# A decoder step on one core: the first group's gather of the last tiles in float32, and sums over partition quarters in quarters of the array

## The chip, the cores and the metric

The kernel runs on one NeuronCore of a Trainium2 chip. The metric is the device time of one execution in microseconds (us). Three runs of the kernel before took 421.94, 422.75 and 424.46 us; the median is 422.75. All rows of before below are of one profiled execution.

## The reference, cut to what matters

One layer of a decoder is computed for 256 prompt tokens and for 8 new tokens, each of which has 1024 cached keys and values in pages.

```python
xn = rmsnorm(x, g_mix); proj = xn @ w_in                     # 1024 -> q | k | v | B | C | h, 512 each
q, k = rope(q), rope(k)                                      # 8 heads of 64
att  = moba_attend(q, k_all, v_all, pos)                     # blocks of 256 keys: own block + top 3 past ones
conv_out, _ = short_conv(c_gate * h_in, conv_prev, conv_w)   # 3 taps
hres = x + concat([att, b_gate * conv_out]) @ w_out          # 1024 -> 1024
hn   = rmsnorm(hres, g_ffn)
# router: best of 4 groups, best 2 of its 8 experts, gates = softmax of the two x probability of the group
h = silu(einsum('td,edf->tef', hn, w_gate)) * einsum('td,edf->tef', hn, w_up) * gates   # 32 experts, 256 wide
y = rmsnorm(hres + einsum('tef,efd->td', h, w_down), g_final)
```

Outputs are the normed rows of both token sets, their keys and values, and the state of the convolution. All is float32.

## The kernel before, in words

Tokens are tiled as tile 0 and tile 1 (128 prompt tokens each) and tile 2 (the 8 new tokens, on 8 partitions). The work ahead of the experts is cut into some 300 named steps. The string `ORDER` lists them; each engine runs its instructions in that order. Q, K, S are steps over the cached keys (gathered by POOL's indirect DMA, multiplied by DVE or POOL, summed by DVE), V over the cached values, `o` the output projection, `H`, `l`, `L` the second norm and the router's logits, `ra` to `re` the five parts of the routing of a tile, `rk` and `oh` the rank of a token within its expert and the one-hot matrix `Pg`, `g` the gather matmuls, `ga` and `gt` copies and transposes of the gathered rows. The first digit behind a letter is mostly the tile.

A product with the 8 new tokens uses TensorE in four column quarters (`mm_quad`, L243): quarter c takes contraction rows of one chunk, and its result is on partitions 32c to 32c+7. The four partial results are then added by a matmul with the 0/1 matrix `sel8`, whose 8 columns pick partitions 0 to 7 of every quarter (`samp_sum` L263, `out_sum` L773; `sq`, `sk`, `sv`, `y0`, `y1` in the order).

The cached values: for token b, `pv_mm` (L709, steps V0 to V7) sums values by probabilities in the four quarters. A DVE multiplication keeps of each of 8 rows its own head (L713). `pv_sum` (L718, X0 and X1) adds the quarters with the matrix `strip`. `pe` adds the token's own value, `as` (L744) transposes.

Expert weights stream through SP's queue into a ring of slots: two `c9` (once `xnT`, `mixT`), nine `rk` (once cached keys and values), four `rw` (once the weights of the projections). Experts are done four at a time, 32 token slots each, in eight groups: `pgt` (gate), `pup` (up, L1149), `px` (gather for the next group), `pyy` (down, L1163), `pz` (scatter). A weight request waits until its slot has been read for the last time, and all behind it in SP's queue wait too. Two `u` tiles of group 0 are loaded in pieces into free small tiles (`load_split`, L1081; their place is taken in step `room`).

The gather of rows is a matmul with the one-hot `Pg`. For it the rows of the residual `yres` are kept as a high part `hn` (float32r, cast by ACT, L820) and a low part `hlo` (the rest, L827: by POOL for tile 2, by DVE for the others), both in an order of columns that makes 8 chunks of every eighth column. Each half of a gather (`PX`, 512 columns) takes a float32r matmul of the high and one of the low part of tiles 0 and 1, and one for tile 2, whose low part lies on partitions 32 to 39 of the same tile:

```python
n = 40 if t == 2 else 128                                   # L985
for low in lows[:1] if t == 2 else lows:
    T.matmul(PX[grp, hf], lhsT=PgS[grp][:n, POS[t]].rearrange("p j s -> p (j s)"), ...
```

Steps `warm0` to `warm2` (L1063) are matmuls without use for the result between the steps that wait for the ranks.

Of the kernel before, what the change touches and what calls it, by code (L numbers as in the profile page):

```python
# [22 lines left out]
H = 8  # L23
# [25 lines left out]
C_ROPE, C_SEL, C_IOTA, C_W4, C_W8, C_WT, C_W = 0, 96, 104, 136, 140, 148, 152  # L49


def _table():
# [12 lines left out]
    t[:, C_WT:C_WT + 4] = [1, 2, 3, 4]  # L65
    return t
# [19 lines left out]
def hymba_step(ctx: ExitStack, tc: tile.TileContext, x_prompt, x_sample, cache_k, cache_v, state_conv,  # L86
# [35 lines left out]
    with tc.manual_schedule():  # L122
# [173 lines left out]
        norm1_T(0)  # L296
        idx = small("idx", [128, 8, 2], I32)
# [28 lines left out]
        strip = small("strip", [128, 64])  # L326
# [27 lines left out]
        def _():  # L354
# [4 lines left out]
            P.memset(strip, 0.0)  # L359
            P.memset(strip[:, 31:32], 1.0)  # L360
# [329 lines left out]
        def _():  # L690
# [5 lines left out]
            for g in range(2):  # L696
                V.tensor_tensor(pvs[g][:, :, :, 0:8], Sd[:, 4 * g:4 * g + 4],
                                bc(rden)[:, 4 * g:4 * g + 4], op=OP.mult)
# [3 lines left out]
        def pv_mm(b):  # L702
            if b == 0:
                Pd["pa"] = ps("pa")
            po = ps("pov", "qb")
            for s in range(2):
                for j in range(4):
                    i = 2 * j + s
                    T.matmul(po[32 * j:32 * j + 32], lhsT=pvs[b // 4][:, b % 4, i, :],  # L709
                             rhs=vslots[2 * b + i // 4][:, i % 4, :], start=s == 0, stop=s == 1,  # L710
                             tile_position=(0, 32 * j))
            mks[b] = c2("mk", [128, 512])
            V.tensor_tensor(mks[b].rearrange("p (h d) -> p h d", h=8), po.rearrange("p (h d) -> p h d", h=8),  # L713
                            sel8[:, :, None].to_broadcast([128, 8, 64]), op=OP.mult)

        def pv_sum(b):
            j = b % 4
            T.matmul(Pd["pa"][32 * j:32 * j + 32], lhsT=strip[:, 31 - b:63 - b], rhs=mks.pop(b),  # L718
                     start=b < 4, stop=b >= 4, tile_position=(0, 32 * j))

        for b in range(8):
            steps[f"V{b}"] = lambda b=b: pv_mm(b)
        steps["X0"] = lambda: [pv_sum(b) for b in range(4)]
        steps["X1"] = lambda: [pv_sum(b) for b in range(4, 8)]

        @step("pe")
        def _():
# [7 lines left out]
            attq = c2("attq", [128, 512])  # L735
            S.copy(attq, Pd["pa"])
            V.tensor_tensor(attq[0:8], attq[0:8], aself, op=OP.add)
            Pd["attq"] = attq
# [57 lines left out]
        def norm2_half(t, k):  # L796
# [20 lines left out]
            V.tensor_tensor(xh[t][:, c0:c0 + m, 0:n], pv_[:, 0:m, 0:n],  # L817
# [591 lines left out]
```

## Time and profile before

| what | us |
|---|---|
| median of three runs | 422.75 |
| the profiled execution, whole | 423.49 |
| its span, first to last instruction | 421.8 |
| PE busy in the span | 382.7 (91%) |
| DVE busy | 196.4 (47%) |
| POOL busy | 104.7 (25%) |
| ACT busy | 92.0 (22%) |

The core moved 155.04 MB by DMA, 119.69 MB of it through SP's queue. A row of a timeline gives start and length in us, engine, line, operation, the tiles written and read, the shape and how many instructions it merges; what stands in brackets is the engine's idle time just before it and what ended it. PE is TensorE's matmuls; in float32 each matmul is two instructions, in float32r one.

### The profile page before, as it was taken

How to read it: one execution, taken by the hardware profiler on the slowest of the kernel's cores; microseconds unless marked ns; L12 is line 12 of the kernel's file. 1: busy time of each engine (PE TensorE's matmuls, PEld its weight loads, DVE VectorE, ACT ScalarE, POOL GpSimd, SP SyncE). 2: the span in 40 equal slices, each digit the busy share in tenths (PEclk: the TensorE clock that was granted, in tenths of full speed). 3: DMA queues.
4: the chain of work that ended last, by engine and by line, in shares of the span. 5: the costliest groups of instructions: out<-in, count | busy, mean ns of one | idle time of the engine just before them, and what ended most of it. 6: DMA issues, size and time to landing. Idle time of an engine off the chain costs nothing.

```text
span 421.8 us, 6576 instructions
## 1 busy us (share of the span) xinstructions
PE 382.7 (91%) x2626; PEld 208.0 (49%) x2626; DVE 196.4 (47%) x384; ACT 92.0 (22%) x232; POOL 104.7 (25%) x103
## 2 busy tenths in 40 slices
PE   7899999999999999987999999888699699799980
PEld 6354346678775334464545554443353364354530
DVE  2148987899764033688234343406015016024054
ACT  4120223164340012241320212111011021011032
POOL 3636888978306001030100000000000000000041
PEclk9899999999999999999899999989889789799996
DMA  7999978869987999949699999999999999999922
GB/s 259 416 373 421 367 292 308 340 220 392 424 358 266 421 429 423 409 204 347 234 413 399 425 427 425 426 428 424 428 427 424 427 427 426 427 427 416 401 99 108
DMA packets 32981, 155.04 MB, mean 368 GB/s; under 512 B 3068, under 2 KB 5322, under 8 KB 17972
## 3 DMA queue, kind: packets, MB, share of 16 engines
q1 hardware_dynamic: 27328, 119.69, 70.1%
q0 software_dynamic: 5008, 33.80, 20.3%
q10 hardware_dynamic: 612, 1.11, 0.7%
q8 instruction: 22, 0.36, 0.3%
q14 instruction: 11, 0.09, 0.1%
HBM read 152.40 MB, written 2.20 MB: 367 GB/s over the span
## 4 chain that ended last, share of the span: by engine, by line
PE 42%; DMA 32%; DVE 13%; issue 7%; POOL 3%; ACT 1%; DVEq 0%; ACTq 0%; SPq 0%; POOLq 0%
DMA u<-in_w_up_dram 14%; DMA g<-in_w_gate_dram 9%; DMA d<-in_w_down_dram 8%; PE py L755 4%; PE pup L1149 4%; PE pov L709 3%; PE acck L238 3%; DVE Sd L480 3%; PE accB L552 3%; PE pgt L1149 3%; PE accq L238 3%; PE pyy L1163 3%; PE accv L238 2%; PE px L987 2%; POOL K L474 1%
## 5 line engine op out<-in xcount | busy, mean ns | idle before, releaser
L1149 PE MATMUL pup<-u,xg 128*32 128x256 f32 x472 | 42.9, 468 | 12.2 <-DMA u<-in_w_up_dram 12.2
L1223 DVE SCALAR_TENSOR_TENSOR sh<-pup,rsl,sh 128x256 f32<-128x256 f32 x8 | 5.3, 666 | 90.2 <-PE pup L1149 83.6
L1126 POOL TENSOR_TENSOR PGw<-Pg,G 128x384 f32<-128x384 f32 x8 | 6.9, 857 | 161.0 <-DVE Pg L976 124.4
L474 POOL TENSOR_TENSOR K<-K,qv 128x2048 f32<-128x2048 f32 x9 | 40.7, 4536 | 6.3 <-DMA K<-in_cache_k_dram,idx 4.5
L480 DVE TENSOR_REDUCE Sd<-K 128x32 f32<-128x2048 f32 x16 | 35.9, 2277 | 4.7 <-POOL K L474 4.6
L1149 PE MATMUL pgt<-g,xg 128*32 128x256 f32 x512 | 32.5, 394 | 3.5 <-DMA g<-in_w_gate_dram 2.4
L1149 PEld LDWEIGHTS pup<-u,xg 128*32 128x32 f32 x472 | 19.2, 133 | 32.0 <-DMA u<-in_w_up_dram 16.3
L1163 PE MATMUL pyy<-d,hT 128*32 128x512 f32 (+1 forms) x272 | 30.9, 579 | 0.6 <-DVE hT L1243 0.6
L755 PE MATMUL py<-wo,mixT 128*128 128x512 f32 (+1 forms) x72 | 29.0, 550 | 1.1 <-DVE yres L760 1.1
L1180 PE MATMUL pz<-Y,PT 128*128 128x512 f32 (+1 forms) x90 | 26.7, 421 | 0.7
L1149 PEld LDWEIGHTS pgt<-g,xg 128*32 128x32 f32 x512 | 16.5, 113 | 18.4 <-DMA g<-in_w_gate_dram 3.8
L1257 DVE TENSOR_TENSOR yres<-yres,pz 128x512 f32<-128x512 f32 (+1 forms) x42 | 25.6, 670 | 0.0
L1172 DVE SCALAR_TENSOR_TENSOR Y<-pyy,gsl,Y 128x512 fp32r<-128x512 f32 (+1 forms) x17 | 12.2, 720 | 25.5 <-ACT Y L1171 25.5
L998 ACT COPY xr<-px 128x512 f32<-128x512 f32 (+1 forms) x16 | 8.8, 557 | 68.0 <-PE px L987 68.0
L987 PE MATMUL px<-hn,Pg 128*128 128x512 f32 (+1 forms) x48 | 21.9, 480 | 0.1
L1171 ACT ACTIVATE Y<-pyy,gsl 128x512 fp32r<-128x512 f32 (+1 forms) x17 | 11.3, 663 | 48.3 <-PE pyy L1163 48.3
L1180 PEld LDWEIGHTS pz<-Y,PT 128*128 128x128 f32 (+1 forms) x90 | 12.1, 154 | 18.0 <-ACT Y L1171 6.4
L303 POOL DMA_INDIRECT V<-in_cache_v_dram,idx x16 | 15.1, 944 | 22.2 <-PE pov L709 18.2
L755 PEld LDWEIGHTS py<-wo,mixT 128*128 128x128 f32 x72 | 13.3, 190 | 13.5 <-issue 11.8
L303 POOL DMA_INDIRECT K<-in_cache_k_dram,idx x16 | 15.7, 982 | 12.4 <-DMA K<-in_cache_k_dram,idx 5.6
L1163 PEld LDWEIGHTS pyy<-d,hT 128*32 128x32 f32 x272 | 8.3, 111 | 17.7 <-issue 16.1
L238 PE MATMUL accq<-wq,xnT 128*128 128x512 f32 x32 | 16.3, 657 | 0.3 <-DVE xnT L221 0.3
(334 smaller groups left out, 612.0 us busy)
## 6 DMA issues: line engine op xcount, KB each, us to landing
g<-in_w_gate_dram SPq DMA_DIRECT2D x32, 1024.0 KB, 19.6
d<-in_w_down_dram SPq DMA_DIRECT2D x28, 1024.0 KB, 19.6
u<-in_w_up_dram SPq DMA_DIRECT2D x25, 1024.0 KB, 19.5
u<-in_w_up_dram SPq DMA_DIRECT2D x9, 512.0 KB, 14.2
wo<-in_w_out_dram SPq DMA_DIRECT2D x4, 1024.0 KB, 15.1
wk<-in_w_in_dram SPq DMA_DIRECT2D x2, 1024.0 KB
wv<-in_w_in_dram SPq DMA_DIRECT2D x2, 1024.0 KB, 30.6
wC<-in_w_in_dram SPq DMA_DIRECT2D x2, 1024.0 KB
```

The source lines that it names most:

```text
L238: T.matmul(acc, lhsT=xnT[:, cc, 128 * t:128 * t + 128], rhs=W[pn, kk][:, c, :], start=cc == 0, stop=cc == 7)
L303: P.indirect_dma_start(out=t, out_offset=None, in_=src, in_offset=bass.IndirectOffsetOnAxis(ap=idx[:, b, hh:hh + 1], axis=0))
L474: P.tensor_tensor(kslots[i], kslots[i], qv[:, None, :].to_broadcast([128, 4, 512]), op=OP.mult)
L480: V.tensor_reduce(Sd[:, b, 4 * hh:4 * hh + 4, :].rearrange("p i h -> p (i h)"), kslots[i].rearrange("p i (h d) -> p (i h) d", h=8), axis=A ...
L552: T.matmul(acc[:, 0:264], lhsT=W[pn, kk][:, c, 128 * m:128 * m + 128], rhs=xnT[:, cc, 0:264], start=cc == 0, stop=cc == 7)
L709: T.matmul(po[32 * j:32 * j + 32], lhsT=pvs[b // 4][:, b % 4, i, :], rhs=vslots[2 * b + i // 4][:, i % 4, :], start=s == 0, stop=s == 1, t ...
L755: T.matmul(po[:, lo:lo + w], lhsT=mixT[:, c, 128 * t:128 * t + 128], rhs=wo[n, c // 4][:, c % 4, lo:lo + w], start=c == 0, stop=c == 7, sk ...
L987: T.matmul(PX[grp, hf], lhsT=PgS[grp][:n, POS[t]].rearrange("p j s -> p (j s)"), rhs=(hn, hlo)[low][t][:n, 4 * hf:4 * hf + 4, :].rearrange ...
L1149: T.matmul(dst[32 * j:32 * j + 32, 0:256], lhsT=xg[:, c, 32 * j:32 * j + 32], rhs=w[:, 256 * k:256 * k + 256], start=c == 0, stop=c == 7, ...
L1163: T.matmul(py[32 * j:32 * j + 32, 0:w], lhsT=hT[:, c, 32 * j:32 * j + 32], rhs=dw[grp, j][:, 1024 * c + a:1024 * c + b], start=c == 0, sto ...
L1180: T.matmul(pz, lhsT=PTS[grp][:, 128 * t:128 * t + NR[t]], rhs=Y[:, i, 0:w], start=start and i == 0, stop=i == 1, skip_group_check=more)
L1257: V.tensor_tensor(yv, yv, pz[:m], op=OP.add)
```

## The change

Six things are changed together.

1. Sums over quarters (`sum_quarters`): the 512 columns are cut into four pieces of 128, and the sum of piece j is done in column quarter j of the array, so that the results stand on partitions 32j to 32j+7. Four copies (or adds) of 128 columns take them back.
2. Four new tokens share one result of the value products: the probabilities of token b of a group of four lie in columns 8(b%4) to 8(b%4)+7 of their 32, and 4 x 16 instructions add into one PSUM tile. One mask multiplication follows for a group. A new step `pa` sums the quarters for both groups; `pe0`, split off `pe`, computes the own value's part earlier; `as` transposes directly.
3. The first group's gather of tiles 2 and 1 reads `yres` itself in float32 (step of 8 elements), with `Pg` as float32, instead of `hn` and `hlo`. The high and low parts of these tiles are made in new steps `hl2`, `hl1` at the end of the order, for the later groups.
4. The order: `re0` comes before the projection of the new tokens, `re2` and `re1` behind the gather, `g00` and `g01` earlier, `R1` ahead of the last scaling of tile 1's transposed rows (`H12` is cut into `H12a`, `H12b`).
5. Three fill steps of two matmuls become one of two and one of one; two matmuls (`keep_warm(2)`) are added behind the first norm's transposes.
6. The two split `u` tiles are requested before the last `g` tile of group 1 instead of behind it.

```diff
@@ ORDER
-cv2 b3 B10 b2 V3 cv0 V0 c2 c3 ov V2 V1 B13 eB1 G25 o010 kvs o000 eB3 G26 eB0 G27 G28 G29 o110 G30 V5 eB2 X0 V4
-o001 V6 H00 G31 o011 V7 H01 X1 pe l00 o100 R0 l01 L0 ra0 rb0 O00 rc0 o101 as rk0 O01 co rd0 z0 z1 y0 oh0 H10 y1 H20
-H21 l20 R2 g00 O20 l21 O21 L2 ra2 rb2 room g01 o111 rc2 l10 O10 o112 H11 R1p H12 rk2 oh2 R1 O11 l11 l12 L1 ra1 rb1 rc1
-g20 warm0 g21 warm1 rk1p rk1 warm2 oh1 O12 rd2 g10h g11h re0 g10l ga0 g11l ga1 re2 gt0 gt1 rd1 re1
+cv2 b3 B10 b2 V3 cv0 V0 c2 c3 ov V2 V1 B13 eB1 G25 o010 kvs pe0 o000 eB3 G26 eB0 G27 G28 G29 o110 G30 V5 eB2 V4
+o001 V6 H00 G31 o011 V7 H01 l00 pa pe o100 R0 l01 L0 ra0 rb0 O00 rc0 o101 as O01 co rd0 re0 z0 z1 rk0 oh0 y0
+y1 H10 g00 H20 g01 H21 l20 R2 l21 L2 ra2 rb2 room o111 rc2 l10 o112 H11 R1p H12a R1 H12b rk2 oh2 l11 l12 L1 ra1 rb1 rc1
+g20 warm0 g21 rk1p rk1 warm1 oh1 rd2 g10 ga0 g11 ga1 gt0 gt1 rd1 re2 re1 hl2 hl1
@@ quarters
+        def sum_quarters(acc, x):
+            for j in range(4):
+                T.matmul(acc[32 * j:32 * j + 8, 0:128], lhsT=sel8, rhs=x[:, 128 * j:128 * j + 128], start=True, stop=True,
+                         tile_position=(0, 32 * j))
...
-            T.matmul(sm[0:8], lhsT=sel8, rhs=part[pn], start=True, stop=True)
-            S.copy(samp[pn], sm[0:8])
+            sum_quarters(sm, part[pn])
+            for j in range(4):
+                S.copy(samp[pn][:, 128 * j:128 * j + 128], sm[32 * j:32 * j + 8, 0:128])
...
         norm1_T(0)
+        keep_warm(2)
@@ values
+            if left[g] == 0:
+                mks[g] = c2("mk", [128, 512])
+                V.tensor_tensor(mks[g].rearrange("p (h d) -> p h d", h=8), po.rearrange("p (h d) -> p h d", h=8),
+                                tab[:, C_HEAD:C_HEAD + 8, None].to_broadcast([128, 8, 64]), op=OP.mult)
...
+        @step("pa")
+        def _():
+            Pd["pa"] = ps("pa")
+            for j in range(4):
+                for g in range(2):
+                    T.matmul(Pd["pa"][32 * j:32 * j + 8, 0:128], lhsT=tab[:, C_TOK + 4 - 4 * g:C_TOK + 12 - 4 * g],
+                             rhs=mks[g][:, 128 * j:128 * j + 128], start=g == 0, stop=g == 1,
+                             tile_position=(0, 32 * j))
...
-                T.matmul(pat[:, 8 * c:8 * c + 8], lhsT=Pd["attq"][:, 128 * c:128 * c + 128], rhs=sel8, start=True,
-                         stop=True)
+                T.transpose(pat[:, 8 * c:8 * c + 8], Pd["attq"][:, 128 * c:128 * c + 128], ident[0:8, 0:8])
@@ output rows of the new tokens
-            T.matmul(po2[0:8], lhsT=sel8, rhs=yq[n], start=True, stop=True)
-            yv = yres[0:8, 2, 512 * n:512 * n + 512]
-            V.tensor_tensor(yv, yv, po2[0:8], op=OP.add)
+            sum_quarters(po2, yq[n])
+            for j in range(4):
+                yv = yres[0:8, 2, 512 * n + 128 * j:512 * n + 128 * j + 128]
+                V.tensor_tensor(yv, yv, po2[32 * j:32 * j + 8, 0:128], op=OP.add)
@@ gather
+                if grp == 0 and t:
+                    n = NR[t]
+                    T.matmul(PX[grp, hf], lhsT=fl(PgS[grp], t, n).bitcast(F32),
+                             rhs=yres[:n, t, :].rearrange("t (p c) -> t c p", c=8)[:, 4 * hf:4 * hf + 4, :],
+                             start=False, stop=t == 1)
+                    continue
...
-            steps[f"warm{i}"] = lambda: fill(2)
+            steps[f"warm{i}"] = lambda i=i: fill(2 - i)
@@ SP's queue
+                    if (grp, nm, j) == (1, "g", 3):
+                        for k in (2, 3):
+                            load_split(0, "u", k, uw, wu_v)
...
-                if (grp, nm) == (1, "g"):
-                    for j in (2, 3):
-                        load_split(0, "u", j, uw, wu_v)
```

## Rows read from the trace of the kernel before

**Rows 1.** The page's 40 slices of the span: GB/s that the DMA engines moved

```profile
GB/s 259 416 373 421 367 292 308 340 220 392 424 358 266 421 429 423 409 204 347 234 413 399 425 427 425 426 428 424 428 427 424 427 427 426 427 427 416 401 99 108
```

**Rows 2.** Busy time by stretch; at the end granted clock, DMA share, GB/s

```profile
184.00:189.00 5.00, 3.86 (x22) 3.17 (x21) 4.69 (x14) 1.03 (x3) 1.67 (x2) 1.00 0.07 26
...
199.00:203.00 4.00, 2.87 (x28) 1.30 (x30) 3.26 (x20) 1.42 (x7) 0.00 (x0) 0.61 0.97 406
203.00:207.00 4.00, 4.00 (x55) 2.50 (x47) 0.71 (x3) 0.59 (x2) 1.02 (x1) 0.96 0.09 28
...
223.00:400.00 177.00, 160.56 (x1432) 83.24 (x1430) 51.52 (x86) 24.01 (x53) 5.00 (x6) 0.92 1.01 424
```

**Rows 3.** Timeline of SP's queue, 174 to 230 us: start, length, request

```profile
175.03 14.14 SPq L1110 DMA_DIRECT2D g<-in_w_gate_dram  x4
...
206.90 13.93 SPq L1110 DMA_DIRECT2D d<-in_w_down_dram  x4
```

**Rows 4.** The chain that ended last, 195 to 245 us: start, length, what

```profile
200.48 5.03 PE pgt L1149 x64
...
207.72 3.59 PE pup L1149 x64
211.31 3.29 PE px L987 x10
...
216.91 3.69 PE pyy L1163 x32
```

**Rows 5.** Timeline of PE

```profile
46.84 1.92 PE L243 MATMUL acck<-wk,xnT 128*32 128x512 f32 x16
...
147.70 1.04 PE L718 MATMUL pa<-mk,strip 128*32 128x512 f32 x8
148.56 1.90 PE L709 MATMUL pov<-V,Pp 128*32 128x512 f32 x16
...
156.37 3.60 PE L755 MATMUL py<-wo,mixT 128*128 128x512 f32 x8
...
162.34 1.37 PE L718 MATMUL pa<-mk,strip 128*32 128x512 f32 x8
...
177.36 1.02 PE L773 MATMUL py<-yq,tab 128*8 128x512 f32 x2
...
186.81 1.99 PE L755 MATMUL py<-wo,mixT 128*128 128x256 f32 x8 [1.14 <-DVE yres L760]
```

**Rows 6.** Timeline of DVE

```profile
182.63 0.24 DVE L862 SCALAR_TENSOR_TENSOR L<-pl,rsb,biasb 8x36 f32<-8x36 f32 x1 [0.67 <-POOL rsb L858]
...
186.20 0.23 DVE L914 SCALAR_TENSOR_TENSOR rcols<-rcols,tab 128x8 f32<-128x8 f32 x1
...
191.83 0.25 DVE L862 SCALAR_TENSOR_TENSOR L<-pl,rsb,biasb 128x36 f32<-128x36 f32 x1 [0.40 <-POOL rsb L858]
...
193.49 0.23 DVE L914 SCALAR_TENSOR_TENSOR rcols<-rcols,tab 128x8 f32<-128x8 f32 x1
...
195.32 0.29 DVE L976 TENSOR_TENSOR Pg<-rka,tab 128x128 fp32r<-128x128 f32 x1
...
198.01 0.74 DVE L1000 COPY xr<-px 128x256 f32<-128x256 f32 x2
```

**Rows 7.** Groups by line and shape, 175 to 192 us: busy, mean ns of one

```profile
L827 POOL TENSOR_TENSOR hn<-yres,hn 8x512 fp32r<-8x512 f32 x2 | 3.0, 1515 | 0.1
...
L827 DVE TENSOR_TENSOR hlo<-yres,hn 128x512 fp32r<-128x512 f32 x1 | 1.1, 1085 | 0.0
...
L827 DVE TENSOR_TENSOR hlo<-yres,hn 128x256 fp32r<-128x256 f32 x1 | 0.6, 610 | 0.0
```

**Rows 8.** Timeline of PE, the first 20 us

```profile
1.44 4.78 PE L287 MATMUL warm<-ident 128*128 128x128 f32 x24 [1.44 <-POOL ident masks.py:199]
...
8.57 3.70 PE L238 MATMUL accq<-wq,xnT 128*128 128x512 f32 x8 [0.35 <-DVE xnT L221]
...
14.55 5.40 PE L238 MATMUL accq<-wq,xnT 128*128 128x512 f32 x8
```

More of the change, by code (lines that the diff above doesn't have):

```diff
@@ L702, in pv_mm @@
         def pv_mm(b):
-            if b == 0:
-                Pd["pa"] = ps("pa")
-            po = ps("pov", "qb")
+            g = b // 4
+            first = g not in Pd
+            if first:
+                Pd[g] = ps("pov", "qb")
+            left[g] -= 1
+            po = Pd[g]
             for s in range(2):
@@ L708, in pv_mm @@
                     i = 2 * j + s
[L709 to L719, printed above, removed]
+                    T.matmul(po[32 * j:32 * j + 32], lhsT=pvs[g][:, b % 4, i, :],
+                             rhs=vslots[2 * b + i // 4][:, i % 4, :], start=first and s == 0,
+                             stop=left[g] == 0 and s == 1, tile_position=(0, 32 * j))
+            if left[g] == 0:
+                mks[g] = c2("mk", [128, 512])
+                V.tensor_tensor(mks[g].rearrange("p (h d) -> p h d", h=8), po.rearrange("p (h d) -> p h d", h=8),
+                                tab[:, C_HEAD:C_HEAD + 8, None].to_broadcast([128, 8, 64]), op=OP.mult)
+        left = [4, 4]
         for b in range(8):
             steps[f"V{b}"] = lambda b=b: pv_mm(b)
-        steps["X0"] = lambda: [pv_sum(b) for b in range(4)]
-        steps["X1"] = lambda: [pv_sum(b) for b in range(4, 8)]
-        @step("pe")
+        @step("pa")
[6 more added lines that the diff above has]
+                             tile_position=(0, 32 * j))
+        @step("pe0")
         def _():
@@ L734, in _ @@
                             ps8[:, :, None].to_broadcast([8, 8, 64]), op=OP.mult)
[L735 to L738, printed above, removed]
+            Pd["aself"] = aself
+        @step("pe")
+        def _():
+            aself = Pd["aself"]
+            attq = Pd["attq"] = c2("attq", [8, 512])
+            for j in range(4):
+                o = slice(128 * j, 128 * j + 128)
+                V.tensor_tensor(attq[:, o], aself[:, o], Pd["pa"][32 * j:32 * j + 8, 0:128], op=OP.add)
         @step("as")
@@ L816, in norm2_half, with norm2_x, norm2_hi, norm2_both @@
                 T.transpose(pv_[:, c, 0:n], y[:, 128 * c:128 * c + 128], ident[:n, :n])
+            return pv_
+        def norm2_x(t, k, pv_):
+            n = NR[t]
+            a, w = COLS[t][k]
+            m, c0 = w // 128, a // 128
             V.tensor_tensor(xh[t][:, c0:c0 + m, 0:n], pv_[:, 0:m, 0:n],
                             gfT[:, c0:c0 + m, None].to_broadcast([128, m, n]), op=OP.mult)
-            p = slice(a // 8, (a + w) // 8)
-            S.copy(hn[t][:n, :, p].rearrange("t c p -> t p c"), y.rearrange("t (p c) -> t p c", c=8))
-        def norm2_lo(t, k):
-            n = NR[t]
-            a, w = COLS[t][k]
-            p = slice(a // 8, (a + w) // 8)
-            (P if t == 2 else V).tensor_tensor(
+            if t == 0:
+                norm2_hi(t, a, w)
+        def norm2_hi(t, a, w):
+            n, p = NR[t], slice(a // 8, (a + w) // 8)
+            S.copy(hn[t][:n, :, p].rearrange("t c p -> t p c"),
+                   yres[:n, t, a:a + w].rearrange("t (p c) -> t p c", c=8))
+        def norm2_both(t):
+            for a in (0, 512):
+                norm2_hi(t, a, 512)
+                norm2_lo(t, a, 512)
+        def norm2_lo(t, a, w):
+            n, p = NR[t], slice(a // 8, (a + w) // 8)
+            V.tensor_tensor(
                 hlo[t][:n, :, p], yres[:n, t, a:a + w].rearrange("t (p c) -> t c p", c=8),
@@ L872, in hymba_step @@
                 steps["R1p"] = lambda: norm2_pre(1)
+                steps.pop("H12")
+                late = []
+                steps["H12a"] = lambda: late.append(norm2_half(1, 2))
+                steps["H12b"] = lambda: norm2_x(1, 2, late[0])
+            if t:
+                steps[f"hl{t}"] = lambda t=t: norm2_both(t)
             steps[f"L{t}"] = lambda t=t: norm2_L(t)
@@ L1054, in hymba_step @@
         for hf in range(2):
-            for low in range(2):
-                steps[f"g1{hf}" + "hl"[low]] = lambda hf=hf, low=low: gather_mm(0, hf, (1,), (low,))
+            steps[f"g1{hf}"] = lambda hf=hf: gather_mm(0, hf, (1,))
             steps[f"ga{hf}"] = lambda hf=hf: gather_rows(0, hf)
@@ L1063, in fill @@
                 T.matmul(w[:, 0:256], lhsT=ident, rhs=yres[:, 0, 0:256], start=True, stop=True)
-        for i in range(3):
-            steps[f"warm{i}"] = lambda: fill(2)
+        for i in range(2):
+            steps[f"warm{i}"] = lambda i=i: fill(2 - i)
         SPLIT = {}
```

18 lines of the change are left out of this document (11 added, 7 removed).

## The prediction

> **What bounds the kernel now.** I began with the page's slices. From the 21st slice (211 us) on the DMA engines move 399 to 428 GB/s almost without a break; before it lie thin slices, above all 204 and 234 GB/s around 180 to 211 us [rows 1]. The table of stretches puts most of that loss in two places: 184 to 189 us with a DMA share of 0.07 and 203 to 207 us with 0.09 [rows 2]. The rest of the kernel streams expert weights at the full rate, so its length is bytes by rate, and the end moves only if this stream starts its unbroken run earlier.
>
> What holds it back is read from SP's queue [rows 3]. Four requests for `g` tiles start at 175.03 us, and the last of them ends 14.14 us later: it waits for the slot of the last output weights. The split `u` tiles of group 0 stand behind it. The four `d` requests of 206.90 end 13.93 us later, at 220.83: the fourth needs a slot that the first group's down projection frees. The chain of waits shows that projection (`pyy`, 216.91 plus 3.69) hanging on `pgt` at 200.48, on `pup` and on `px`, all on PE back to back [rows 4]. So the end follows the start of the first `pgt`, and the price of the change is how much earlier that comes. PE and the chain through DVE in front of it, 145 to 200 us, are what counts. DMA would cap the gain only far on: between 184 us and the fourth `d` it has ten tiles of 1024 KB to move (two `u` of the first group, one `g`, four `u`, three `d`), 10.49 MB at 424 GB/s [rows 2], 24.7 us, so it could be there at 208.7 us against 220.8 now: 12 us.
>
> **The change part by part.** Signs: minus is earlier.
>
> *Sums of the attention results.* PE now runs eight full-width instructions at 147.70 (0.86 us until the next at 148.56) and eight at 162.34 in 1.37 us, 0.1 of it beside the next [rows 5]: 2.1 us, part of it a wait for the last mask product. After, sixteen short instructions (128 columns) do both, and the router logits `l00` stand ahead of them and cover the wait. Sixteen quarter-array instructions of 512 columns take 1.92 us [rows 5], four abreast, so 0.43 us for four; a 128-column set is then 0.11 us if four run abreast. Here the two token groups of a quarter follow each other, so the bounds are 0.43 us (all abreast) and 1.7 us (in line, 0.11 each); I take 0.9. Gain 2.1 - 0.9, **-1.2** (-0.5 to -1.7). Six of eight mask products go from DVE, and PE doesn't wait for them: nothing. The four transposes in place of eight matmuls in `as` end before DVE has copied their neighbours: nothing.
>
> *Sums over quarters.* `sq`, `sk` and `sv` lie before 108 us, where DVE and POOL go through the cached keys; PE gets ahead there only to wait: nothing, with four small copies on ACT in place of one. `y0` and `y1` are on the path: 1.02 us each [rows 5] becomes 0.3 to 0.95, I take 0.4. Against that, four adds of 128 columns stand for one of 512; a 128-column DVE instruction is 0.29 us [rows 6], 1.2 at most for four. And `re0`, 1.5 us of DVE work, now comes ahead of them. Together -1.0 to +0.6; I take **-0.3**. The Trainium skill ("TensorEngine Tiling (Array Packing)", Performance Considerations, PSUM Bottleneck) warns that after a fourfold faster TensorE the copies out of PSUM may be the limit. By it the adds alone set this step and the sum would be about 1 us longer; the rows do not show such a split result, so none of that is in the sum.
>
> *The low parts of the last tiles leave the path.* POOL's two subtractions (1515 ns each [rows 7]) go to the end and to DVE. While they ran, the routing of the eight new tokens on DVE took from 182.63 (L862) to 186.20 (L914), 3.57 us; the same steps of tile 1, without POOL, take 191.83 to 193.49, 1.66 us [rows 6]. PE's last output matmuls wait for the add queued behind that routing (1.14 us of idle time before 186.81 [rows 5]). The 1.9 us become **-1.8** for the end of those matmuls. Then the order: the reciprocal root starts ahead of the last transposed copy, and a subtraction of 256 columns (610 ns [rows 7]) is gone from DVE. From the end of `o112` (188.80 [rows 5]) to the logits at 191.83 [rows 6] were 3.0 us; I get 2.2, so **-0.8** (0 to -1.2).
>
> *From the last one-hot to the first `pgt`.* `Pg` ends at 195.61 [rows 6], `pgt` starts at 200.48 [rows 4]: 4.87 us. It holds four px instructions, two of which wait for the subtraction, the copies `xr` on DVE at 198.01 [rows 6], delayed by gate weights of tile 0, transposes, and `xg` behind those of tile 2. After, one float32 matmul of two passes per half: a 512-column pass is 0.43 us (eight in 3.60, starts to starts 3.44 [rows 5]), so 0.86 where two fp32r instructions took 0.66 (ten in 3.29 [rows 4]). The gate weights of tiles 0 and 2 leave. Chain: px 0.9, copy 0.4 beside the other half, second px 0.85, copy 0.35, transposes and `xg` 0.4: 2.9 us. **-2.0** (-2.4 to +2). The two gathers of tile 2 and the two fill matmuls between them fit into the 2.9 us in which DVE routes tile 1 (0.86 for each of the three pairs, 0.3 for ranks), without slack.
>
> *Clock.* From 200 to 203 us PE is granted 1.2 instead of 2.4 GHz (0.61 in the mean of 199 to 203 [rows 2]), after a stretch in which it waited for DVE; `pgt` takes 5.03 us where `pup` takes 3.59 [rows 4]. With the waits gone from just ahead, I expect 2.4: **-1.4** (0 to -1.4).
>
> *What is given back.* The casts and subtractions of two tiles now run after `xg`, four on ACT and four on DVE, 1.1 us each [rows 7], and must end before the second group's px, some 9 us later. They fit, with DVE late by **+0.3** (0 to +1). The two matmuls after the first transposes are four instructions of 0.2 us (24 in 4.78 [rows 8]) in a gap of 0.35 us: **+0.4** for everything behind, if nothing absorbs it. The second `q` product, at 14.55, takes 5.40 us for eight instructions, the first 3.70 [rows 8], which looks like the lower clock again. If the shift prevents that, 1.7 us come back; the added work itself lies ahead of the first product, so I count 0.
>
> *The moved requests.* The split `u` tiles, six DMAs on SP, go ahead of the last `g`. If their slots were late, that `g` and every later weight would wait behind them; the slots are free once `y1` is done, near 179 us, and the `g` can't go before `o112` anyway, near 185. They fill the dry stretch at 184 us, which by the above is not what binds: 0.
>
> Sum: -1.2 - 0.3 - 1.8 - 0.8 - 2.0 - 1.4 + 0.3 + 0.4 = -6.8 us. The profiled execution took 423.49 us (span 421.8 and 1.7 around it), 0.74 above the median of the runs: 416.7 from the one, 416.0 from the other. I say 416.5.
>
> **Rivals.** *Strided reads on PE.* The float32 gather reads `yres` with a step of 32 bytes, which no matmul of before does. DVE does it in the subtractions: 1085 ns for 512 and 610 for 256 columns [rows 7], so 1.86 ns for each element more. If PE is held to that pace, a pass is 0.95 us and a gather 1.9 in place of 0.86. The two of tile 2 delay the ranks by 2.1, the two of tile 1 the tail by 2.1: 420.7. For it: DVE's contiguous 256-column copies `xr` take 0.74 us for two [rows 6], 0.37 each, so the step costs DVE 1.6 times. Against: PE's float32 passes take an element only every 0.84 ns as they are, and hold nothing else up between two of them. The Trainium skill ("SBUF — State Buffer", Door 1: The DMA port swizzle) says that reads which hit a 16-byte line only once pay a penalty; it names no engine as exempt and gives no price, and the DVE rows agree with it.
>
> *Slower.* The same place at POOL's pace: 1515 ns for 512 elements [rows 7]. A gather is 3.0 us, four add 8.7: 425.2. It decides from 2.56 us a gather on, 1.28 a pass, where the four eat the 6.8. Against: POOL shared its time with DVE there.
>
> *The quarters run in line.* The sums then keep their length (1.7 and twice 0.95): +0.8 and +1.1, 418.4. Against: the sixteen quarter instructions in 1.92 us do run abreast [rows 5].
>
> **How the numbers follow.** Forecast 0.57, quarters in line 0.10, strided at DVE's pace 0.24, slower 0.09. A median can tell about 0.5% from no change, 420.6 to 424.9. The forecast's own range is 414.7 (the early fall of the clock prevented) to 418; the range takes in the strided case: 414.3 to 421.2. Faster: 0.57 + 0.10 and four tenths of 0.24 (its time lies at the bound), 0.77; same 0.14; slower 0.09.
>
> **What would show it.** `pgt` of the first group starts near 194 and takes 3.6 us; float32 px passes of 0.43 us apart from each other (0.95 means the rival); quarter sums of 0.4 us; routing of tile 2 in 1.7 us; the fourth `d` request near 214, and 424 GB/s from there to the same tail. I am wrong if `pgt` comes earlier and the end does not, or if the end moves by what happens before 108 us.

## The result, and the profile after

The changed kernel takes 425.18 us (median of 17 runs, 424.03 to 427.19) beside 423.28 us for the kernel before (17 runs on the same chip): a ratio of 1.0056, 95% interval 1.0038 to 1.0074. It is slower by 1.9 us, where I forecast 416.5 and a range to 421.2. The profiled execution has a span of 423.2 us (421.8 before). The ratios below leave out runs over 1.5% slower than the fastest of their kernel; the medians of f4, g2 and h3 still have two, one and one of them, and are 423.18, 420.49 and 421.64 without.

Much came as predicted. The sums over quarters shrank from 1.02 to 0.41 us and the two sums of attention results from 2.1 to 0.64 ([rows 5]; `pa` below). With POOL's subtractions gone from beside it, the routing of tile 2 takes the 1.66 us that I had foreseen (3.57 in [rows 6]), and the logits of tile 1 are there at 189.37 instead of 191.83. Timeline of DVE, kernel after, the counterparts of [rows 6], and the adds that take the quarter sums back:

```profile
177.86 2.41 DVE L799 TENSOR_TENSOR yres<-yres,py 8x128 f32<-8x128 f32 x8
...
182.65 0.24 DVE L902 SCALAR_TENSOR_TENSOR L<-pl,rsb,biasb 8x36 f32<-8x36 f32 x1 [0.67 <-POOL rsb L898]
...
184.31 0.23 DVE L961 SCALAR_TENSOR_TENSOR rcols<-rcols,tab 128x8 f32<-128x8 f32 x1
...
189.37 0.25 DVE L902 SCALAR_TENSOR_TENSOR L<-pl,rsb,biasb 128x36 f32<-128x36 f32 x1
```

Timeline of PE, kernel after:

```profile
163.68 0.64 PE L741 MATMUL pa<-mk,tab 128*8 128x128 f32 x16
...
177.31 0.41 PE L267 MATMUL py<-yq,tab 128*8 128x128 f32 x8
...
189.28 2.08 PE L1035 MATMUL px<-yres,Pg 8*128 8x512 f32 x2
191.28 2.08 PE L1116 MATMUL warm<-yres,ident 128*128 128x256 f32 x4
193.29 2.18 PE L1035 MATMUL px<-yres,Pg 8*128 8x512 f32 x2
...
196.72 3.87 PE L1035 MATMUL px<-yres,Pg 128*128 128x512 f32 x4
200.41 1.54 PE L1070 MATMUL pxt<-ident,xr 128*128 128x128 f32 x8
201.87 3.66 PE L1202 MATMUL pgt<-g,xg 128*32 128x256 f32 x64
...
207.50 0.91 PE L1190 MATMUL pgs<-ones__71,PGw 128*128 128x1 f32 x6 [0.60 <-POOL PGw L1179]
```

This is where the lead goes: two float32 passes take 2.08 to 2.18 us, not 0.86, and tile 1's four take 3.87. The ranks wait behind them, and `pgt` starts at 201.87, later than the 200.48 of [rows 4]. It runs at full speed (3.66), ends level with before, and PE then waits 0.60 us for POOL's `PGw`. So the last of the four `d` requests goes out at 221.52, 0.7 us later than in [rows 3] (220.83). Timeline of SP's queue:

```profile
174.75 2.04 SPq L1166 DMA_DIRECT2D g<-in_w_gate_dram  x3
...
206.92 14.60 SPq L1166 DMA_DIRECT2D d<-in_w_down_dram  x4
```

Stretches, after, with the columns of [rows 2], and last the one of before that belongs to the last of them:

```profile
184.00:189.00 5.00, 4.46 (x31) 3.73 (x29) 3.59 (x18) 1.02 (x4) 0.64 (x2) 1.00 1.03 399
191.00:200.00 9.00, 9.00 (x16) 3.79 (x16) 2.69 (x14) 0.76 (x4) 0.00 (x0) 0.50 0.69 284
203.00:207.00 4.00, 3.90 (x57) 2.43 (x49) 3.62 (x19) 4.00 (x9) 1.23 (x1) 1.00 0.08 23
224.00:395.00 171.00, 154.09 (x1342) 79.24 (x1342) 50.72 (x84) 24.01 (x53) 4.99 (x6) 0.92 1.01 420
```

```profile
224.00:395.00 171.00, 155.20 (x1360) 80.38 (x1360) 50.02 (x83) 24.01 (x53) 5.00 (x6) 0.92 1.01 425
```

Three things stand out. The dry stretch at 184 us is filled; what that is worth by itself no run shows (I forecast nothing). The granted clock is 0.50 (the 1.2 GHz level) from 190.6 to 200.8 us, for the gather but its first 1.3 us, where before it stayed at 1.00 until 199.9. And the stream of weights, untouched by the change as I read it, runs at 420 GB/s; before, the same stretch has 425.

### The profile page after: what moved, and what is told of

Read it like the earlier page. It is cut to its first block, busy times and chain, and to the rows that moved or that the text cites. A ratio compares the mean times of both kernels' runs of the same rounds, so it can differ in the third digit from the quotient of the medians.

```text
span 423.2 us, 6631 instructions
## 1 busy us (share of the span) xinstructions
PE 384.9 (91%) x2652; PEld 209.2 (49%) x2652; DVE 195.5 (46%) x388; ACT 93.2 (22%) x239; POOL 102.3 (24%) x99
## 4 chain that ended last, share of the span: by engine, by line
DMA 44%; PE 28%; issue 12%; DVE 8%; POOL 6%; ACT 1%; SPq 0%; DVEq 0%; POOLq 0%; ACTq 0%
DMA u<-in_w_up_dram 14%; DMA d<-in_w_down_dram 12%; DMA g<-in_w_gate_dram 9%; DMA K<-in_cache_k_dram,idx 5%; PE py L778 4%; PE pup L1202 4%; PE pov L723 3%; PE accB L560 3%; DVE Sd L488 3%; PE pyy L1216 3%; POOL K L482 2%; PE px L1041 2%; DMA uq<-in_w_up_dram 2%; POOL K L314 2%; PE pgt L1202 2%
## 5 line engine op out<-in xcount | busy, mean ns | idle before, releaser
L1041 PE MATMUL px<-hn,Pg 128*128 128x512 f32 (+1 forms) x44 | 20.1, 480 | 0.0
L484 DVE TENSOR_TENSOR K<-K,qb 128x2048 f32<-128x2048 f32 x7 | 16.0, 2280 | 0.7 <-DMA K<-in_cache_k_dram,idx 0.6
```

The lines of the kernel that those rows point to most:

```text
L484: V.tensor_tensor(kslots[i], kslots[i], qbs[b][:, None, :].to_broadcast([128, 4, 512]), op=OP.mult)
```

## The experiments

All medians stand beside runs of the kernel before on the same chip (422.4 to 423.3). "Sum to pup" is the time in one profile from the second quarter sum (`y1`) to the first `pup`, the stretch that the gather sets. In the four rows that do the work of the kernel before (before, f2, g4, i3) it goes from 27.4 to 28.8: in before and g4 the clock falls just ahead of `pgt`, which costs 1.3 to 1.4 us, in f2 and i3 it does not.

| kernel | us | ratio to before, 95% | GB/s, 224 to 395 us | sum to pup, us |
|---|---|---|---|---|
| before | 423.28 | | 425 | 28.8 |
| after | 425.18 | 1.0056 (1.0038 to 1.0074) | 420 | 30.4 |
| e1 contiguous | 424.25 | 1.0026 (0.9990 to 1.0061) | 420 | 29.2 |
| e3 no keep | 425.11 | 1.0060 (1.0032 to 1.0088) | 420 | 30.4 |
| e4 sums | 424.59 | 1.0032 (1.0002 to 1.0061) | 420 | 29.9 |
| f1 after, 32 bytes | 426.59 | 1.0084 (1.0053 to 1.0115) | 420 | 30.4 |
| f2 before, 32 bytes | 426.55 | 1.0085 (1.0057 to 1.0113) | 418 | 27.4 |
| f3 sums, 32 bytes | 424.32 | 1.0030 (1.0008 to 1.0051) | 420 | 29.7 |
| f4 natural order, 32 bytes | 423.55 | 0.9993 (0.9968 to 1.0017) | 420 | 28.4 |
| g1 after, old addresses | 422.03 | 0.9978 (0.9953 to 1.0003) | 425 | 29.6 |
| g2 natural order, old addresses | 420.59 | 0.9937 (0.9911 to 0.9963) | 425 | 28.4 |
| g3 sums, old addresses | 421.23 | 0.9952 (0.9927 to 0.9977) | 425 | 28.5 |
| g4 before, 512 bytes | 423.14 | 0.9998 (0.9974 to 1.0023) | 425 | 28.7 |
| h1 fill first | 419.86 | 0.9910 (0.9875 to 0.9945) | 425 | 27.7 |
| h2 late subtractions | 422.08 | 0.9968 (0.9941 to 0.9995) | 425 | 29.5 |
| h3 tile 2 late | 421.78 | 0.9957 (0.9926 to 0.9988) | 424 | 27.0 |
| i1 full rows | 417.25 | 0.9855 (0.9830 to 0.9880) | 424 | 25.3 |
| i2 zero rows | 417.29 | 0.9877 (0.9846 to 0.9908) | 424 | 25.3 |
| i3 before, 256 bytes | 422.72 | 0.9992 (0.9972 to 1.0012) | 425 | 27.4 |

**Stride or clock.** e1:

```diff
-                             rhs=yres[:n, t, :].rearrange("t (p c) -> t c p", c=8)[:, 4 * hf:4 * hf + 4, :],
+                             rhs=yres[:n, t, 512 * hf:512 * hf + 512],
```

> The changed kernel, but the float32 gather of the first group reads 512 contiguous columns of yres instead of 512 columns with a step of 32 bytes (same rows, same number of instructions; the columns come in another order than tile 0's, so the first group's slots hold mixed-up columns, and the experts' results are not the reference's). In the profile of the changed kernel the first pair of passes took 2.08 us, the four of tile 1 3.87 us, and the granted clock was 0.50 from about 191 to 200 us. Theory 'stride': TensorE reads a step of 32 bytes at about 0.95 us a 512-column pass, also at the full clock. Then here the first pair takes 0.9 us, the second too, ranks of tile 1 no longer wait for PE (prk near 193 instead of 195.7), pgt starts 3 to 5 us earlier than in the changed kernel (197 to 199 us), and the time falls by 2 to 4 us against the changed kernel, to 421 to 423. Theory 'clock': the step costs nothing, the passes are slow because the clock fell to half. Then the four passes of tile 1 still take 3.4 to 3.9 us at a clock of 0.50, pgt starts within 1 us of 201.9, and the time stays near 425.

`pgt` came at 199.77, 2.1 us earlier (1.0 of it is there at `y1` already, 176.98 for 177.97), but the clock fell all the same (from 189.1 us on) and the four passes of tile 1 took 3.62. Each theory got half of it, and the time, 424.25, hardly moved.

e2, the same pass at the full clock:

```diff
+            probe_mm(8, y[:, 0:512])
+            probe_mm(8, y.rearrange("t (p c) -> t c p", c=8)[:, 0:4, :])
+            probe_mm(8, y[:, 0:512])
+            probe_mm(4, y.rearrange("t (p c) -> t c p", c=4)[:, 0:2, :])
+            probe_mm(4, y.rearrange("t (p c) -> t c p", c=2)[:, 0, :])
```

> The changed kernel with extra float32 matmuls, whose results nobody reads, put on TensorE behind the quarter sums of y0, near 177 us, where the granted clock was 1.00: 8 instructions of 512 contiguous columns, 8 with a step of 32 bytes, 8 contiguous, 4 of 512 columns with a step of 16 bytes, 4 of 512 with a step of 8 bytes, 8 contiguous. Each float32 instruction is two passes. Its time says nothing; the durations do. Theory 'stride': contiguous passes take 0.43 us each, those with a step of 32 bytes 0.9 to 1.0 us each while the clock is still 1.00; a step of 16 bytes is between, 8 bytes nearer to 0.43. Theory 'clock': all take 0.43 us as long as the clock is 1.00. The third open point: if the clock falls to 0.5 within or just behind the strided stretch and not behind the contiguous ones, the strided reads themselves bring it down.

Weight loads stand one ahead of each pass, so the distance of their starts is the length of a pass. Timeline of PE's weight loads, e2: contiguous, then steps of 32, 16 and 8 bytes:

```profile
181.25 0.19 PEld L1121 LDWEIGHTS probe<-yres,ident 128*128 128x128 f32 x1 [0.24 <-issue]
181.68 0.19 PEld L1121 LDWEIGHTS probe<-yres,ident 128*128 128x128 f32 x1 [0.24 <-issue]
...
186.56 0.21 PEld L1121 LDWEIGHTS probe<-yres,ident 128*128 128x128 f32 x1 [0.71 <-issue]
187.48 0.21 PEld L1121 LDWEIGHTS probe<-yres,ident 128*128 128x128 f32 x1 [0.71 <-issue]
...
208.08 0.21 PEld L1121 LDWEIGHTS probe<-yres,ident 128*128 128x128 f32 x1 [0.69 <-issue]
208.98 0.21 PEld L1121 LDWEIGHTS probe<-yres,ident 128*128 128x128 f32 x1 [0.69 <-issue]
...
213.94 0.19 PEld L1121 LDWEIGHTS probe<-yres,ident 128*128 128x128 f32 x1 [0.26 <-issue]
214.39 0.19 PEld L1121 LDWEIGHTS probe<-yres,ident 128*128 128x128 f32 x1 [0.26 <-issue]
```

0.43 us contiguous, 0.92 with a step of 32 bytes, 0.90 with 16, 0.45 with 8; the granted clock is 1.00 over all 46 us, so strided reads alone don't bring it down. "Stride" holds at the full clock. With the clock at one half (1.2 GHz) four contiguous passes take 3.41 us up to the next instruction (194.78 to 198.19 in e1), 0.85 each, and four strided ones 3.69 (after, 196.72 to 200.41), 0.92 each, the same as at the full clock. So the costs don't add: either of them alone takes most of the gain. The Trainium skill ("SBUF — State Buffer", Door 1: The DMA port swizzle) asks for two hits on a 16-byte line; the break between a step of 8 and of 16 bytes agrees with it.

**The added warm-up.** e3 drops `keep_warm(2)`.

> The changed kernel without the two added matmuls behind the first transposes. If the 0.9 us by which acck started later in the changed kernel, and the 1.4 us by which the cached keys' chain on DVE ran late from 76 us on, come from these instructions, then acck starts near 21.8 us, pov near 130.2, and the time falls by 0.4 to 1.4 us, to 424 to 424.8. Rival: the shift comes from the start (first x tile and warm-up were 0.4 us later already) or from the order of the work, then nothing moves by more than 0.3 us, and the time stays at 425.

425.11, no change; the rival was right.

**The sums alone, and a stream that is slow in all of these.** e4 is the kernel before with parts 1 and 2 of the change only.

> The kernel before with the two sums of the change alone: the sums over partition quarters in array quarters (q, k, v, y0, y1), and four new tokens sharing one attention result; gather, order of the tail, requests and warm-up as before. By the prediction the end comes 1.5 us earlier (-0.5 to -2.3), a time of 421.8 where the kernel before has 423.3. Rival: the sums on PE were hidden behind DVE and POOL, the four adds in place of one take back what is won (2.4 us of adds in the profile of the changed kernel); then no change, 423.3, or up to 0.6 later.

424.59, 0.3% slower than before, by an interval that just excludes no change, although the stream of weights behind the gather was not touched. Its stream has 420 GB/s, as e1's and e3's. What all share is memory: the table grew by 80 bytes a partition, which take up 96, and `strip` (256) went: 160 bytes less, so every weight slot moved, the first of them from 40960 to 40800 bytes.

f1 and f2 put 32 unused bytes ahead, into the kernel after and into the kernel before:

```diff
         tab = small("tab", [128, C_W])
+        pad = small("pad", [128, 8])
```

> The changed kernel with an unused tile of 32 bytes a partition behind the table, so that yres, the weight slots and mixT, which in the changed kernel start 32 bytes off a multiple of 64, start on one, as in the kernel before. Four kernels with the wider table and without the strip tile (after, e1, e3, e4) streamed 420 GB/s from 224 to 395 us, the kernel before 425 to 426. Theory 'address': the rate comes from where the slots lie. Then this one streams 425 to 426 GB/s, 171 us at 420 become 169, and the time falls by 1.5 to 2.5 us, to 422.7 to 423.7, the level of the kernel before; the gather and the clock stay as they were (pgt of the first group near 202, clock 0.50 from 191 to 200). Rival 'order': the rate comes from the order of requests or from the wider table's load in DRAM. Then it stays at 420 and the time at 425.

> The kernel before with the same unused tile of 32 bytes a partition and nothing else: its slots now start 32 bytes off a multiple of 64. Theory 'address': 420 GB/s from 224 to 395 us instead of 425, and the time rises by 1.5 to 2.5 us to 424.5 to 425.5, with no change of the work at all. Whether the cached keys' chain before 108 us also gets later, as it did by 1.4 us in the changed kernel, is open: 'address' says yes if the transfers set that stretch. Rival: nothing moves, 423.

f2 settles that addresses matter: the same work, 32 bytes further, takes 3.5 us more and streams 418 GB/s. f1 refutes the multiple of 64 that I had expected to suffice. f3 (e4 with this pad) says the same as f1: I expected 425 GB/s and 421.8, and it has 420 and 424.32. g1 puts the slots where they were (160 bytes), g3 does so for the sums alone, g4 and i3 move the kernel before's slots to 40448 and 40704:

> The changed kernel with an unused tile of 160 bytes a partition behind the table: all slots of the ring then lie at the addresses that they have in the kernel before (40960, 49152, ..., multiples of 8192). f2 showed that 32 bytes more cost the kernel before 3.5 us and bring its stream from 425 to 418 GB/s; f1 showed that a multiple of 64 (40832) doesn't give the rate back. Theory 'slot lines': the rate needs the slots at a coarser multiple, which 40960 is and 40800 and 40832 are not. Then 425 GB/s here, acck and the cached keys' chain up to 0.5 and 1.1 us earlier, and a time 2 to 3.5 us under the changed kernel's 425.2: 421.7 to 423.2. Rival: the rate of the changed kernel comes from something else that it has (wider table, requests); then 420 GB/s and 425.

> The kernel before with the two sums of the change alone, and the slots at the addresses of before (160 bytes). By 'slot lines' 425 GB/s, and what is left is what the sums are worth by themselves: 421.8 by the prediction (-1.5), 423 if they were hidden. By the rival 424.3.

> The kernel before with one constant tile of 512 bytes (the causal mask) moved behind everything else, so that the slots start at 40448, a multiple of 512 and not of 1024. If a multiple of 512 is enough, 425 GB/s and 423.0, no change; if it takes more, 418 to 420 GB/s and 425 to 426.5, as with the 32 bytes.

> The kernel before with one constant tile of 256 bytes (strip) moved behind everything else, so that the slots start at 40704, a multiple of 256 and not of 512; yres stays where it was. Slots at 40960 and 40448 (multiples of 512) streamed 425 GB/s, at 40800, 40832 and 40992 (multiples of 32, 128 and 32) 418 to 420. If a multiple of 256 is enough, 425 GB/s and 423.0; if it takes 512, 418 to 420 GB/s from 224 to 395 us and 425 to 426.5.

The stretch 224 to 395 us of f2, f1, g1, g4 and i3, one row each, in this order:

```profile
224.00:395.00 171.00, 152.35 (x1339) 77.65 (x1332) 49.85 (x83) 24.13 (x53) 5.00 (x6) 0.93 1.01 418
```

```profile
224.00:395.00 171.00, 155.19 (x1342) 79.09 (x1342) 50.63 (x84) 24.00 (x53) 4.99 (x6) 0.91 1.01 420
```

```profile
224.00:395.00 171.00, 155.88 (x1356) 80.75 (x1348) 49.39 (x82) 24.01 (x53) 4.99 (x6) 0.92 1.01 425
```

```profile
224.00:395.00 171.00, 155.11 (x1352) 79.39 (x1351) 51.17 (x85) 24.04 (x53) 5.00 (x6) 0.92 1.01 425
```

```profile
224.00:395.00 171.00, 155.91 (x1356) 80.75 (x1348) 49.30 (x82) 24.00 (x53) 5.00 (x6) 0.91 1.01 425
```

Slots at multiples of 256, 512 or 8192 stream 425 GB/s; at 40800, 40832 and 40992 (multiples of 32, 128 and 32) 418 to 420. DMA's busy share is 1.01 in all: the same bytes keep the engines busy longer. No run moves the slots alone to a bad address; that it is they, and not another tile behind the pad, is argued from what flows in this stretch, requests for `g`, `u` and `d` into the slots (71.37 of f2's 71.55 MB). The Trainium skill ("DMA: Bandwidth & Descriptors", How a descriptor splits into AXI transactions) tells, of what a descriptor reads, of pieces that start at 256-byte addresses; here it is the side written that moved, and the multiple agrees with these rows. At the addresses of before, the change is worth -0.2% (g1) and the sums alone -0.5% (g3).

**Reading in natural order.** f4 and g2 keep `hn` and `hlo` in the order of the columns, read 512 contiguous ones, and reorder in the copies:

```diff
-            S.copy(rows_[:, 0:w], px[:, 0:w])
+            S.copy(rows_[:, :, 64 * hf:64 * hf + w], px[:, :, 0:w])       # px seen as "s (p c) -> s c p"
```

> The changed kernel with the tile of 32 bytes, and with the gather's rows in their natural order: hn and hlo are written and read contiguously, the float32 gather reads 512 contiguous columns, and the copies xr (ACT and DVE) put the columns into the order that the transposes want. The probe gave 0.43 us for a contiguous pass at the full clock and 0.92 with a step of 32 bytes; e1, with contiguous reads and the clock at 0.50, started pgt 2.1 us earlier than the changed kernel. Expected: pgt of the first group near 200 (2 us earlier than in f1; the strided copies give back 0.2 to 0.5), the clock still at 0.50 from about 189, and a time of 421 to 422, 1.5 to 2 us under f1. If the clock stays at 1.00, pgt near 197 and 419. Rival: the fill of the slots behind 206 us sets the end whatever the gather does; then the same as f1.

> f4 (contiguous gather in natural order) with the unused tile of 160 bytes instead of 32. By 'slot lines' 425 GB/s and 2 to 3.5 us less than f4's 423.6: 420 to 421.6, 0.4 to 0.7% under the kernel before. By the rival 423.6.

g2 came as expected. f4 gained more on f1 than the 1.5 to 2 us expected (3.0), and still lies above the 421 to 422 that I gave, since f1 itself had not sped up. The clock still fell (0.66 in the mean of 187 to 197 us in g2).

**What brings the clock down.** h1 puts the fills of `warm0` ahead of `g20`; h2 issues `hl2` and `hl1` behind `slot_maps`; h3 does four fills, the ranks, and tile 2's gathers last.

> g2 (contiguous gather, slots at the addresses of before; pgt at 198.60 us, 22.4 us after the second quarter sum at 176.16; the clock at 0.50 from 189.3 to 196.1) with the two fill matmuls of 256 columns put ahead of the first gather of tile 2 instead of behind it. Theory 'clock': the fall hangs on what TensorE did just ahead, transposes, 36-column logits and 8-row gathers with gaps; with full passes in that place the clock stays at 1.00, the four passes of tile 1 take 1.75 us in place of 3.52, the tile 2 pair 0.9 in place of 2.07, pgt comes 2.5 to 3.5 us earlier and the time falls by as much, to 417.5 to 418.5. Rival: the fall isn't moved by where the fills stand (the same work is done), the time stays at 420.6, or is 0.5 us later, because the fills delay the ranks.

> g2 with the casts and subtractions of tiles 2 and 1 issued behind the weighted one-hots (PGw on POOL, and the matmuls that wait for it) instead of ahead. In the changed kernel PGw took 1.68 us beside DVE's subtractions, and PE stood 0.60 us before pgs. Theory: PGw takes about 0.9 us again, the gap of 0.6 us ahead of pgs goes, pup starts 0.5 to 0.7 us earlier after pgt, and the time is 0.5 to 0.7 under g2's 420.6: 420. Rival: the subtractions come late for the second group's gather and give it back there: 420.6 or up to 0.5 more.

> g2 with four fill matmuls (eight passes of 256 columns) ahead of the ranks of tile 1 and tile 2's gathers behind its one-hot, directly ahead of tile 1's. Theory 'clock': the eight passes hold the clock at 1.00; the gathers then take 1.8 us of float32 passes for tile 2 and 1.75 for tile 1 in one go, where g2 needed 2.07 + 3.52 after its fall; pgt 1 to 2 us earlier than in g2, time 418.6 to 419.6. Rival: the clock falls all the same, then tile 2's passes at half clock lie on the path too, pgt 1.5 to 2.5 us later, 422 to 423.

h1 is 0.7 us under g2 (intervals that overlap), less than hoped: the clock fell later, at 192 us, but fell. h2's `PGw` took 0.83 us as expected, yet from `prs` to `pup` that gave only 0.17 us (2.21 for g2's 2.38), and the second group's gather waited 1.01 us for its one-hot behind the subtractions. h2 is 1.5 us over g2, with intervals that overlap, and in its profile the clock was low for 10 us where g2 has 7, so what the later subtractions cost by themselves is open. h3 kept the clock at 1.00 in its profile and, by times and mean clocks, not in all runs: five, with a mean clock of 0.948 to 0.960, took 417.7 to 419.7, six others, at 0.940 to 0.948, 421.6 to 422.9, and one, at 0.939, 424.1. In the profiles of h2, g2 and h1 the fall comes within the passes over tile 2's 8 rows, between them and 1.8 us behind them. These passes are not all that can bring it: in e4 and g3, whose gathers are those of the kernel before, the clock is at 0.50 from 180.2 to 187.0 us and from 180.6 to 184.0, behind waits and transposes of 8 rows. i1 and i2:

```diff
-                    T.matmul(PX[grp, hf], lhsT=fl(PgS[grp], t, n).bitcast(F32),          # g2, n = 8 for tile 2
-                             rhs=yres[:n, t, 512 * hf:512 * hf + 512],
+                    u = 0 if t == 2 else t                                                # i1
+                    T.matmul(PX[grp, hf], lhsT=fl(PgS[grp], u, 128).bitcast(F32),
+                             rhs=yres[:, u, 512 * hf:512 * hf + 512],
...
+        V.memset(yres[:, 2, :], 0.0)                                                      # i2, on h1, with n = 128
+        P.dma_start(yres[0:8, 2, :], x_sample.rearrange("b o d -> b (o d)"))
```

> g2 with the two float32 gathers of tile 2 (8 rows, four passes) replaced by gathers of tile 0's 128 rows, the same number of passes at the same place (tile 0 is added twice and the new tokens are left out of the first group, so the result is another). In g2, h2 and h1 the clock fell 1.8, 0.6 and 3.8 us behind the start of these 8-row passes (from 189.3, 188.3, 192.0 us on, with starts at 187.47, 187.76, 188.20); in h3, which did them later, it stayed at 1.00. Theory 'thin passes': passes over 8 of 128 rows bring the clock down; with 128 rows it stays at 1.00 from 187 to 197, tile 1's four passes take 1.75 us, pgt comes 2.5 to 3.5 us earlier than in g2 (22.4 us after the second quarter sum there; 19 to 20 here), and the time is near 418. Rival: the fall hangs on the gaps and the 36-column logits ahead; then it falls as in g2, pgt 22.4 us after the sum, and the time is 420.6.

> h1 (fills first, contiguous, addresses of before; 419.9) with tile 2's gather over all 128 rows: rows 8 to 127 of that tile are set to zero on DVE at the start, and its rows are loaded on POOL's queue behind that. By 'thin passes' the clock stays at 1.00 through the gather, tile 1's passes take 1.75 us where h1 took 3.15, pgt 3.66 where h1 took 4.39: 1.5 to 2.5 us under h1, 417.5 to 418.5. By the rival, 419.9, and up to 1 us more for the later load of the new tokens at the start.

The stretch 187 to 197 us of g2 and of i1 (clock 0.66 and 1.00; DVE's busy time shows that the chain got further):

```profile
187.00:197.00 10.00, 9.48 (x21) 3.77 (x20) 4.57 (x24) 1.14 (x5) 0.14 (x2) 0.66 0.81 336
```

```profile
187.00:197.00 10.00, 8.43 (x53) 4.79 (x57) 6.85 (x36) 2.33 (x11) 0.45 (x2) 1.00 0.87 358
```

And PE's timeline in i2, beside the one of after above:

```profile
187.59 1.88 PE L1038 MATMUL px<-yres,Pg 128*128 128x512 f32 x4
...
190.76 1.98 PE L1038 MATMUL px<-yres,Pg 128*128 128x512 f32 x4
193.66 1.09 PE L1073 MATMUL pxt<-ident,xr 128*128 128x128 f32 x8 [0.92 <-DVE xr L1057]
194.84 3.66 PE L1205 MATMUL pgt<-g,xg 128*32 128x256 f32 x64
```

i1 differs from g2 in nothing but the rows (and the sum that they give), and takes 3.3 us less, with intervals far apart; with 128 rows for 8 the clock stays up through the gather (it falls at 202 us, in `pup`). i2 computes what the reference does, at 417.29, 1.2% under the kernel before. It is 2.6 us under h1, with intervals that overlap. Two of its six runs took 419.5 and 419.8 at a mean clock of 0.947 and 0.948, the other four 416.2 to 417.9 at 0.957 to 0.959, so its clock, too, seems not to hold in every execution.

## Why the prediction was wrong

**The bound** was read rightly: the end follows the first `pgt` and the stream behind it. In eleven profiles whose stream has 424 or 425 GB/s, 199.4 to 201.5 us lie between the issue of the fourth `d` request and the end of the span, in the other eight of the table, with 418 to 420, 201.6 to 204.3. In i2's profile that request goes out at 213.92, where I had said near 214, 6.9 us earlier than in [rows 3], and the span is 7.7 us shorter.

**The sums** (-1.2 and -0.3) held in total, not in their parts: g3 gives -0.48% (-0.73 to -0.23), 2.0 us. From the second block of value products to the output products of the new tokens, before needs 43.79 us and f3, which has the sums alone, 42.12. That is -1.7 for the attention sums, the far end of the range. Timeline of PE, before and f3:

```profile
130.11 3.64 PE L709 MATMUL pov<-V,Pp 128*32 128x512 f32 x32
...
173.90 3.64 PE L243 MATMUL py<-wo,mixT 128*32 128x512 f32 x32
```

```profile
131.10 3.64 PE L723 MATMUL pov<-V,Pp 128*32 128x512 f32 x32
...
173.22 3.64 PE L247 MATMUL py<-wo,mixT 128*32 128x512 f32 x32
```

They ran four abreast (0.64 us where in line would be 1.7); the rival "in line" is out. The two sums `y0` and `y1` gave no gain: from `y0` to the logits of tile 2, f3 needs 5.58 us and before 5.27, +0.3 where I had -0.3. The rule of the Trainium skill ("TensorEngine Tiling (Array Packing)", Performance Considerations, PSUM Bottleneck) that the copies out of PSUM may set such a step did bear: from `y1` to those logits there are 4.66 us in f3 and 4.68 in the changed kernel (177.97 to 182.65), 3.73 before (178.90 to 182.63), and the eight adds take 2.41 us. Of the "about 1 us" that I named and left out of the sum, 0.6 was there.

**Low parts and order** (-1.8 and -0.8) held: from the logits of tile 2 to those of tile 1 6.72 us in place of 9.20, -2.5.

**The step that failed** is "From the last one-hot to the first `pgt`". Counted from the logits of tile 1, before needs 8.65 us to `pgt`, after 12.50: +3.9 where the sum has -2.0. I took 0.43 us for a float32 pass from a contiguous row; the strided read takes 0.92 (e2). That was the rival at 0.24, whose figure, 0.95 from DVE's rows, was nearly right; its time, 420.7, was not, for addresses and clock came on top. What I held against it, that PE's float32 passes take an element only every 0.84 ns anyway, doesn't help against a read that needs 1.8 ns (0.92 us for 512). The rival *Slower* names 425.2 and 425.18 was measured, which is luck: it rests on passes of 1.5 us. Reading contiguously, with the copies that then reorder, gives 1.4 us (g1 to g2, intervals that just overlap). Even in i2, with contiguous reads and the clock up, the step is worth -0.7 (7.91 us), not -2.0; PE stands 0.92 us in it for the reordering copies, where I had 0.35 for a copy.

**The clock** (-1.4) went the other way. I expected 2.4 GHz once the waits ahead of `pgt` were gone, and looked at gaps alone. The changed kernel has fewer of them and its clock fell 9 us earlier; what falls together with it are the 8-row passes, which the change put in the place of 40-row ones. With 128 rows there the fall in the gather is gone, 3.3 us (g2 to i1). `pgt` itself took 3.66 us for 5.03, since the clock was back by then. But the 1.4 us belonged to the profiled execution and not to the kernel before: f2 and i3 do the same work, and their `pgt` takes 3.66 us too, without the change. Timeline of PE in f2:

```profile
201.66 3.66 PE L1150 MATMUL pgt<-g,xg 128*32 128x256 f32 x64 [1.13 <-DVE xg L1019]
```

So a saving was counted that one execution showed and others do not need.

**What is given back** behind `pgt` was +0.7 in the changed kernel (from `prs` to `pup` 2.88 us for 2.21) and +0.2 in i2 (2.38), where I had +0.3; the 0.4 for `keep_warm(2)` was nothing that e3 could show. The value products of the changed kernel's profile are 1.4 us late already (131.48 for 130.11), but in the four profiles that do the work of before they start anywhere from 130.11 to 131.27, so my last sign of being wrong, an end moved by what happens before 108 us, can't be read from it.

**A term was missing**, and it is as large: the addresses, 3.2 us (after to g1, 425.18 to 422.03, intervals apart). I priced a wider table at nothing and took "424 GB/s from there to the same tail" as fixed. Of the 3.2, 171 us at 420 in place of 425 GB/s are 2.0; in g1's profile the clock also came back 2.4 us sooner and `y1` came 0.5 us earlier, and whether the addresses do that too is open (`y1` starts anywhere from 178.90 to 180.05 in the four profiles that do the work of before). At equal addresses the change as it stands is worth -0.2% (-0.47 to +0.03): no difference that can be told.

So the forecast failed by three separate things, 3.2 us of addresses (after to g1), 1.4 of strided reads (g1 to g2) and 3.3 of clock (g2 to i1). That they leave 417.3 of 425.2 is no test, since these steps end at i1's 417.25 by construction; i2, which has the right result, is at 417.29, with the fills first besides. That this is within 1 us of the forecast is in part luck: the gather's step gave 1.3 us less than I counted, and the 1.4 of `pgt` was not there to be had.

## What to carry to other kernels

A change of small tiles moves every large one behind them: compare the rate of the unchanged streams first, and keep the slots of big transfers at multiples of 256 bytes, which was enough here. Price a matmul by its access pattern as well as its columns: a step of 16 or 32 bytes doubled a float32 pass at the full clock here. And where a matmul over few rows stands in for one over many in a thin stretch, look at the granted clock behind it; 128 rows in place of 8 saved 3.3 us here (g2 to i1), and rows of zeros did as well (i2). And before a slow stretch of one profile is counted as a gain, see whether other executions of the same work have it.

## What the hardware showed that I had not expected

- A shift of all that lies behind the table, the slots among it, by 32 bytes, with no other difference, cost the kernel before 0.85% (0.57 to 1.13).
- On TensorE a float32 read with a step of 8 bytes is as good as free (0.45 us for 0.43), with 16 bytes it costs all that 32 do (0.90 and 0.92).
- A strided float32 pass takes 0.92 us at the full and at the half clock alike, a contiguous one 0.43 and 0.85.
- Not settled: why 32 bytes (40992) are no better than 96 or 128 past a multiple of 256, and why the clock held in some executions of h3 and not in others.
